# One encoder layer by Strassen quarters: a finished quarter is queued two steps later, the first W2 chunk reloads a tile, and the last chunk runs in another order

## The chip, the cores and the metric

The kernel runs on one core of a Trainium2 chip. The metric is the time of one execution on the device in microseconds (us). Times are given as a median of several runs; a profile is one more execution, taken by the hardware profiler.

## What is computed

One layer of a bidirectional encoder, 512 tokens of width 2048, all in float32. Only the second half matters here: the gate, the two feed-forward matrices and the last layer norm.

```python
mix = concat([rms_norm(A), rms_norm(B)]) @ w_o
h   = layer_norm(ALPHA * x + mix, ln1_g, ln1_b)
ff  = square(relu(h @ w1)) @ w2                  # w1: 2048 x 8192, w2: 8192 x 2048
ple = (p @ w_ple) * sigmoid(h @ w_ple_gate)      # w_ple_gate: 2048 x 2048
out = layer_norm(ALPHA * h + ff + ple, ln2_g, ln2_b)
```

## The kernel before

**Number format.** A float32 product is made of three matmuls (L653, L655, L656): each operand is split into a rounded part and the remainder (`wh`, `wl` for weights; `sh`, `sl` for the other side). ScalarE (ACT) makes the rounded part, VectorE (DVE) the remainder (L598, L599 for weights).

**Chunks and steps.** The three big matrices are worked off in chunks, each of them one call of `strassen` (L602): two chunks for the gate, eight for W1, then four pairs (`m` = 0 to 3, `c` = 0, 1) for W2; eighteen in all. A chunk multiplies a 512 x 1024 block by a 1024 x 1024 block with Strassen's (Winograd's) seven products instead of eight. Each block is cut into four quarters; product `p` (1 to 7) is accumulated over four depth slices `k` (0 to 3). A pair (p, k) is a **step**: 12 matmuls of 512 columns. The 28 steps of a chunk run in the order of `STEPS` (L804), counted here from 0 to 27. The results gather in three PSUM tiles `a`, `b`, `c` (`CHAIN`); when a product's last slice is done, `read` adds the PSUM tile into the output quarters. A quarter is finished after product 3, 7, 4 or 2 (`LAST`): in `STEPS` these end at step 18 (first half of the rows, second half of the columns), 19 (second, second), 25 (second, first) and 27 (first, first).

**Weight factors.** `factor(p, k)` (L609) loads the four weight quarters of slice k (each a 512 KB DMA) and forms the sums that the seven products need: at p = 1 it loads the first quarter (tag `r`), the second one (tag `q`, or `g` if `hold`) and the fourth one (tag `k`, issued from the POOL queue; all others come from the SP queue). At p = 5 it forms second minus first (L616) and the next sum (L617); at p = 3 it loads the fourth quarter again and, without `hold`, the second one again (L624), and forms their difference (L625). With `hold` (all W2 chunks) the second quarter stays in a `g` tile from p = 1 to p = 3 and is loaded once. At p = 2 and p = 4 the third quarter is loaded and the last sum formed (L634).

**Buffers.** `WB` (L803) gives the number of buffers of each tag, 512 KB each: `r` 4, `q` 2, `k` 4, `wh` 3, `wl` 3, `c` 3, `g` 4. `q` also takes the tiles `qs` through which the other side's factors for W2 come back from the scratch tensor `s_d` (`f_factors`, L576, L584); ten of them are placed at steps 3 to 21 of the chunk before a pair, four (`LATE`, L807) at steps 12, 14, 16 and 18 of the pair's first chunk. `g` takes the blocks `f` of the squared activations in W1, and the gate's side loads.

**What happens with a finished quarter.** `quarters(done)` (L661) calls `done` as soon as the quarter's last read is issued (L673). In the gate, `gated` (L683) loads two blocks, applies the sigmoid, transposes on TensorE (L694) and writes to `z_d`. In W1, `squared` (L705) transposes the quarter on TensorE into the tile `pt` (eight transposes, L710), applies relu and square on ACT, forms the sums that Strassen needs on the other side (L720 to L727) and writes seven factors to `s_d`. In W2 the results are added to `z_d` by DMA, but for the last pair (`m` = 3), where `last_sum` (L735) loads `z_d`, adds the PSUM tiles (L743) and takes the layer norm's statistics (L746).

**The end.** `finish(th, z)` (L761) works on one half of the rows (two tiles of 128 rows): per tile it loads the other columns, combines the statistics (L767), takes the reciprocal root by a short chain of tiny DVE operations (L269 to L277), applies two fused operations to three pieces (L777, L778) and stores them. In the last chunk it is called after product 4 (step 25, second half of the rows) and after product 2 (step 27, first half).

**What sets the order.** The framework's scheduler writes each engine's instruction stream, the DMA queues' too, when the program is built. It goes by program order among the instructions that it expects to be ready at that moment, so a load can be issued well ahead of its step as soon as a buffer of its tag is free, and an instruction that is not expected to be ready is passed by later ones. On the chip each engine then runs its stream strictly in order.

Of the kernel before, what the change touches and what calls it, by code (L numbers as in the profile page):

```python
# [11 lines left out]
F32 = mybir.dt.float32  # L12
# [5 lines left out]
P = 128  # L18
# [20 lines left out]
def block_kernel(ctx: ExitStack, tc: tile.TileContext, xT, pT, positions, w_in, w_o, w_gate, w_ple,  # L39
# [562 lines left out]
    def strassen(src, sg, read, hold=False, between={}):  # L602
# [4 lines left out]
        b11, b12, b21, b22, t2 = {}, {}, {}, {}, {}  # L607

        def factor(p, k):  # L609
            if p == 1:  # L610
                b11[k] = w_load(src(k, 0), "r")
                b12[k] = w_load(src(k, 1), "g" if hold else "q")
                t2[k] = w_load(src(k, 3), "k")
                return b11[k]
            if p == 5:
                nc.vector.tensor_tensor(b11[k], b12[k], b11[k], op=ALU.subtract)  # L616
                nc.vector.tensor_tensor(t2[k], t2[k], b11[k], op=ALU.subtract)  # L617
                return b11[k]
            if p == 6:
                return t2[k]  # L620
            if p == 3:
                b22[k] = w_load(src(k, 3), "r")
                if not hold:
                    b12[k] = w_load(src(k, 1), "q")  # L624
                nc.vector.tensor_tensor(b12[k], b22[k], b12[k], op=ALU.subtract)  # L625
                return b22[k]
            if p == 7:
                return b12[k]
            if p == 2:
                b21[k] = w_load(src(k, 2), "r")  # L630
                return b21[k]
            if k not in b21:
                b21[k] = w_load(src(k, 2), "r")
            nc.vector.tensor_tensor(t2[k], b21[k], t2[k], op=ALU.subtract)  # L634
            return t2[k]

        for n, (p, k) in enumerate(STEPS):
# [3 lines left out]
            if p == 2 and k in b21:  # L641
                wh, wl = w_split(b21[k])
            else:
                wh, wl = w_split(factor(p, k))
# [15 lines left out]

    def quarters(done):  # L661

        c = {}

        def read(p, b):
# [6 lines left out]
            if p in LAST:  # L672
                done(*q, c[q])  # L673
# [58 lines left out]
    bs = [st.tile([P, 4, nc.vector.BN_STATS_DIM], F32, name=f"bs{t}", bufs=1) for t in range(NQ)]  # L732
    gb = []

    def last_sum(c):  # L735
        z = {}
# [4 lines left out]
        def read(p, b):  # L741
            q = READ[p]
            nc.vector.tensor_tensor(z[q], z[q], b, op=ALU.add)  # L743
            if p in LAST:
                for t in range(2):
                    nc.vector.bn_stats(bs[2 * q[0] + t][:, 2 * c + q[1]], z[q][:, t])  # L746
                if c == 0:
                    nc.gpsimd.dma_start(z_d[q[0], q[1]], z[q])
            if c == 1 and p == 5:
# [7 lines left out]
            if c == 1 and p in (4, 2):  # L757
                finish(1 if p == 4 else 0, z)
        return read

    def finish(th, z):  # L761
        for i in range(2):
# [3 lines left out]
            mv = st.tile([P, nc.vector.BN_AGGR_DIM], F32, name="mv")  # L766
            nc.vector.bn_aggr(mv, bs[t])  # L767
            v = st.tile([P, 1], F32, name="v")
            nc.vector.tensor_scalar(v, mv[:, 1:2], LN_EPS, None, op0=ALU.add)
            r = st.tile([P, 1], F32, name="r")  # L770
            rsqrt(r, v)
            rows = slice(t * P, (t + 1) * P)
            for y, n, k in ((x.rearrange("p n s -> p (n s)"), 0, 2), (z[th, 0][:, i], 2, 1), (z[th, 1][:, i], 3, 1)):
# [3 lines left out]
                nc.vector.scalar_tensor_tensor(y, y, mv[:, 0:1], g[:, o], op0=ALU.subtract, op1=ALU.mult)  # L777
                nc.vector.scalar_tensor_tensor(y, y, r, b[:, o], op0=ALU.mult, op1=ALU.add)  # L778
# [4 lines left out]
    for m in range(NM):  # L783
# [5 lines left out]
        for c in range(2):  # L789
# [5 lines left out]
            strassen(lambda k, q, m=m, c=c: w2[m, c, q, k], sf, read if more else last_sum(c), True, mid)  # L795
# [11 lines left out]
LATE = {2: (12, 16), 4: (14, 18)}  # L807
CHAIN = {1: ("a", True), 6: ("a", False), 7: ("a", False), 4: ("a", False), 5: ("b", True), 3: ("b", False),
# [93 lines left out]
```

## Time and profile before

| | |
|---|---|
| median of 3 runs | 2268.99 us (2266.04 to 2269.82) |
| the profiled execution | 2262.9 us |
| its span, first to last instruction | 2261.1 us |
| TensorE (PE) busy | 2144.7 us, 95% |
| VectorE (DVE) busy | 1612.5 us, 71% |
| ScalarE (ACT) busy | 1061.6 us, 47% |
| mean granted TensorE clock | 0.982 |

Times in the trace count from the start of the span. The eighteen chunks start at 740.22 (gate), 919.59 (W1) and 1576.63 (W2); the last matmul starts at 2232.30. Matmuls are pipelined: the profile gives each one a modelled duration of about 0.39 us, while they start about 0.23 us apart, so a busy TensorE still can lose time, and the distance between starts tells more than the busy share. The granted clock has two levels here, 1.0 (2.4 GHz) and 0.5 (1.2 GHz).

### The profile page before, as it was taken

The numbers are of one execution on the slowest core, as the hardware profiler recorded it, in microseconds if no ns is written. First come the engines' busy times: TensorE is split into PE (matmuls) and PEld (weight loads), VectorE is DVE, ScalarE is ACT, GpSimd is POOL, SyncE is SP. The second block draws the span as 40 slices with busy tenths as digits, with TensorE's granted clock in tenths as the row PEclk, the third lists the DMA queues.
The fourth block names the chain that finished last, engine by engine and source line by source line (L and its number), as shares of the span: only waits on it lengthen the run. The fifth ranks groups of instructions, "written<-read, shape, count | busy, mean of one in ns | idle before, by whom it ended". The sixth has DMA issues, their size and how long they took to land.

```text
span 2261.1 us, 26072 instructions
## 1 busy us (share of the span) xinstructions
PE 2144.7 (95%) x9672; PEld 1757.3 (78%) x9672; DVE 1612.5 (71%) x1969; ACT 1061.6 (47%) x1372; POOL 124.3 (5%) x192
## 2 busy tenths in 40 slices
PE   9999999999995799999999999998899999999994
PEld 7888888888884588888888888776777787787783
DVE  7666655566475988776876877777677776777787
ACT  5554444343234444454555455455445555455331
POOL 0000000000003000000000000000011011001000
PEclk9999999999998899999999999999999999999997
DMA  6212212224225775565565566567669679678552
GB/s 225 75 66 76 84 66 84 84 100 138 99 88 209 269 271 202 202 230 180 190 229 177 196 214 204 190 221 250 202 186 285 182 206 277 181 210 289 187 197 82
DMA packets 124544, 401.60 MB, mean 178 GB/s; under 512 B 13024, under 2 KB 24288, under 8 KB 124416
## 3 DMA queue, kind: packets, MB, share of 16 engines
q1 hardware_dynamic: 88544, 285.51, 36.7%
q0 software_dynamic: 23584, 85.06, 13.4%
q10 hardware_dynamic: 12288, 29.36, 3.5%
q8 instruction: 76, 1.25, 0.2%
q14 instruction: 52, 0.43, 0.1%
HBM read 329.63 MB, written 70.25 MB: 177 GB/s over the span
## 4 chain that ended last, share of the span: by engine, by line
PE 76%; DMA 9%; DVE 9%; issue 3%; ACT 2%; DVEq 0%; SPq 0%; ACTq 0%
PE u L72 9%; PE u L71 9%; PE a L656 9%; PE u L73 9%; PE a L653 9%; PE a L655 8%; DMA wr<-in_w 5%; PE b L656 4%; PE b L653 4%; PE b L655 4%; DVE wl L599 4%; PE c L656 2%; PE c L653 2%; PE c L655 2%; DMA qs<-s_d 2%
## 5 line engine op out<-in xcount | busy, mean ns | idle before, releaser
L598 ACT ACTIVATE wh<-wr 128x1024 fp32r<-128x1024 f32 x288 | 303.8, 1059 | 345.2 <-PE a L655 194.0
L599 DVE TENSOR_TENSOR wl<-wr,wh 128x1024 fp32r<-128x1024 f32 x288 | 350.2, 1221 | 96.5 <-ACT wh L598 93.3
L64 ACT ACTIVATE wh<-raw 128x512 fp32r<-128x512 f32 x216 | 135.7, 629 | 282.2 <-PE u L72 267.3
L65 DVE TENSOR_TENSOR wl<-raw,wh 128x512 fp32r<-128x512 f32 x216 | 150.8, 699 | 160.8 <-ACT wh L64 129.0
L598 ACT ACTIVATE wh<-wk 128x1024 fp32r<-128x1024 f32 x144 | 152.6, 1060 | 179.3 <-PE b L655 89.5
L71 PE MATMUL u<-xh,wh 128*128 128x512 f32 x576 | 227.8, 395 | 5.6 <-ACT xh L64 5.6
L73 PE MATMUL u<-xh,wl 128*128 128x512 f32 x576 | 225.7, 392 | 0.0
L72 PE MATMUL u<-xl,wh 128*128 128x512 f32 x576 | 225.6, 392 | 0.0
L599 DVE TENSOR_TENSOR wl<-wk,wh 128x1024 fp32r<-128x1024 f32 x144 | 175.6, 1222 | 66.2 <-ACT wh L598 66.1
L634 DVE TENSOR_TENSOR wk<-wr,wk 128x1024 f32<-128x1024 f32 x72 | 88.2, 1224 | 97.1 <-DMA wr<-in_w 91.2
L653 PE MATMUL a<-wh,s1h 128*128 128x512 f32 x288 | 114.8, 399 | 30.7 <-DMA qh<-h_d 29.3
L71 PEld LDWEIGHTS u<-xh,wh 128*128 128x128 f32 x576 | 108.9, 189 | 27.1 <-ACT xh L64 5.6
L653 PE MATMUL b<-wh,s5h 128*128 128x512 f32 x288 | 116.6, 405 | 12.1 <-ACT wh L598 12.1
L73 PEld LDWEIGHTS u<-xh,wl 128*128 128x128 f32 x576 | 108.7, 189 | 22.7
L656 PE MATMUL b<-wl,s5h 128*128 128x512 f32 x288 | 117.2, 407 | 9.3 <-DVE wl L599 9.3
L72 PEld LDWEIGHTS u<-xl,wh 128*128 128x128 f32 x576 | 108.9, 189 | 22.0 <-DVE xl L65 0.4
L656 PE MATMUL c<-wl,s2h 128*128 128x512 f32 x288 | 113.3, 393 | 6.0 <-DVE wl L599 5.7
L656 PE MATMUL b<-wl,s3h 128*128 128x512 f32 x288 | 113.5, 394 | 4.1 <-DVE wl L599 3.9
L656 PE MATMUL a<-wl,s1h 128*128 128x512 f32 x288 | 114.8, 399 | 2.4 <-DVE wl L599 2.4
L655 PE MATMUL b<-wh,s5l 128*128 128x512 f32 x288 | 115.5, 401 | 0.0
L653 PE MATMUL a<-wh,s7h 128*128 128x512 f32 x288 | 112.6, 391 | 2.9 <-ACT wh L598 2.9
L656 PE MATMUL a<-wl,s7h 128*128 128x512 f32 x288 | 113.0, 392 | 1.2 <-DVE wl L599 1.1
(243 smaller groups left out, 4933.4 us busy)
## 6 DMA issues: line engine op xcount, KB each, us to landing
wr<-in_w SPq DMA_DIRECT2D x192, 512.0 KB, 4.0
raw<-in_w_in SPq DMA_DIRECT2D x64, 512.0 KB, 3.6
wq<-in_w SPq DMA_DIRECT2D x64, 512.0 KB, 3.7
wk<-in_w POOLq DMA_DIRECT2D x64, 512.0 KB, 4.8
qs<-s_d SPq DMA_DIRECT2D x56, 512.0 KB, 4.9
z_d<-ev POOLq DMA_DIRECT2D x42, 512.0 KB, 7.2
raw<-in_w_o SPq DMA_DIRECT2D x32, 512.0 KB, 3.4
s_d<-f POOLq DMA_DIRECT2D x32, 512.0 KB, 5.2
```

The source lines that it names most:

```text
L64: nc.scalar.activation(hi, src, AF.Copy)
L65: nc.vector.tensor_tensor(lo, src, hi.bitcast(F32), op=ALU.subtract)
L71: nc.tensor.matmul(o, wh, ah, start=start, stop=False)
L72: nc.tensor.matmul(o, wh, al, start=False, stop=False)
L73: nc.tensor.matmul(o, wl, ah, start=False, stop=stop)
L598: nc.scalar.activation(hi, t, AF.Copy)
L599: nc.vector.tensor_tensor(lo, t, hi.bitcast(F32), op=ALU.subtract)
L634: nc.vector.tensor_tensor(t2[k], b21[k], t2[k], op=ALU.subtract)
L653: nc.tensor.matmul(o, sh[:, i, x], wh[:, c], start=first and k == 0 and j == 0, stop=False, skip_group_check=skip)
L655: nc.tensor.matmul(o, sl[:, i, x], wh[:, c], start=False, stop=False, skip_group_check=skip)
L656: nc.tensor.matmul(o, sh[:, i, x], wl[:, c], start=False, stop=k == 3 and j == 1, skip_group_check=skip)
```

## The change

1. **Two steps later.** `quarters` no longer calls `done` at once; it puts it on a list `after`, and `strassen` runs it at the start of the second step from there. The quarters that end at steps 25 and 27 are thus handled at step 27 and at step 1 of the next chunk. `last_sum` does not use the list.
2. **Loads by need.** `factor` loads the second and fourth quarters at p = 5 instead of p = 1, two to three steps later in program order, in all chunks, and keeps every tile in a dictionary so that the products may come in another order.
3. **The first W2 chunk** (`m` = 0, `c` = 0) runs without `hold`: its second quarter is loaded into `q` at p = 5 and loaded again into `q` at p = 3 (four more DMAs of 512 KB).
4. **The last chunk** runs in the order `ENDS`: after step 11 come products 2, 7 and 4, then 3 and the rest of 2. The second half of the rows is finished at step 21, the first half at steps 26 and 27. The fourth quarter is loaded a third time there (four more DMAs of 512 KB).
5. **Statistics** of a half's two row tiles are combined in one chain of tiny operations instead of two (`row_stats`).

```diff
@@ strassen @@
-        b11, b12, b21, b22, t2 = {}, {}, {}, {}, {}
+        b11, b12, b21, b22, t1, t2, t3, t4 = ({} for _ in range(8))
+
+        def get(b, k, q, tag):
+            if k not in b:
+                b[k] = w_load(src(k, q), tag)
+            return b[k]
+
+        def sum4(k):
+            if k not in t4:
+                t4[k] = t2[k]
+                nc.vector.tensor_tensor(t4[k], get(b21, k, 2, "r"), t2[k], op=ALU.subtract)
+            return t4[k]
+
+        def sum3(k, b):
+            x = b12[k] if hold else w_load(src(k, 1), "q")
+            nc.vector.tensor_tensor(x, b, x, op=ALU.subtract)
+            t3[k] = x
+            return x
 
         def factor(p, k):
             if p == 1:
-                b11[k] = w_load(src(k, 0), "r")
-                b12[k] = w_load(src(k, 1), "g" if hold else "q")
-                t2[k] = w_load(src(k, 3), "k")
-                return b11[k]
+                return get(b11, k, 0, "r")
             if p == 5:
-                nc.vector.tensor_tensor(b11[k], b12[k], b11[k], op=ALU.subtract)
-                nc.vector.tensor_tensor(t2[k], t2[k], b11[k], op=ALU.subtract)
-                return b11[k]
+                spent = k in b11
+                x, y = get(b11, k, 0, "r"), get(b12, k, 1, "g" if hold else "q")
+                get(t2, k, 3, "k")
+                t1[k] = x if spent else y
+                nc.vector.tensor_tensor(t1[k], y, x, op=ALU.subtract)
+                nc.vector.tensor_tensor(t2[k], t2[k], t1[k], op=ALU.subtract)
+                return t1[k]
...
             if p == 3:
-                b22[k] = w_load(src(k, 3), "r")
-                if not hold:
-                    b12[k] = w_load(src(k, 1), "q")
-                nc.vector.tensor_tensor(b12[k], b22[k], b12[k], op=ALU.subtract)
-                return b22[k]
+                x = w_load(src(k, 3), "r")
+                if k not in t3:
+                    sum3(k, x)
+                return x
             if p == 7:
-                return b12[k]
+                return t3[k] if k in t3 else sum3(k, w_load(src(k, 3), "r"))
...
-        for n, (p, k) in enumerate(STEPS):
+        for n, (p, k) in enumerate(steps or STEPS):
+            for w in list(after):
+                w[0] -= 1
+                if w[0] == 0:
+                    after.remove(w)
+                    w[1]()
             for f in between.get(n, ()):
                 f()
@@ quarters @@
             if p in LAST:
-                done(*q, c[q])
+                after.append([2, lambda: done(*q, c[q])])
@@ last_sum and finish @@
+    def row_stats(th):
+        mv = st.tile([P, 2, nc.vector.BN_AGGR_DIM], F32, name="mv")
+        for i in range(2):
+            nc.vector.bn_aggr(mv[:, i], bs[2 * th + i])
+        v = st.tile([P, 2], F32, name="v2")
+        nc.vector.tensor_scalar(v, mv[:, :, 1], LN_EPS, None, op0=ALU.add)
+        r = st.tile([P, 2], F32, name="r2")
+        rsqrt(r, v)
+        return mv, r
...
+            if p in LAST:
+                ends.append(q[0])
+                if c == 1 and ends.count(q[0]) == 2:
+                    finish(q[0], z)
...
-            if c == 1 and p in (4, 2):
-                finish(1 if p == 4 else 0, z)
@@ W2 loop @@
-            strassen(lambda k, q, m=m, c=c: w2[m, c, q, k], sf, read if more else last_sum(c), True, mid)
+            strassen(lambda k, q, m=m, c=c: w2[m, c, q, k], sf, read if more else last_sum(c), m + c > 0, mid,
+                     STEPS if more or c == 0 else ENDS)
...
+ENDS = STEPS[:12] + ((2, 0), (7, 0), (7, 1), (7, 2), (7, 3), (2, 1), (4, 0), (4, 1), (4, 2), (4, 3),
+                     (3, 0), (2, 2), (3, 1), (3, 2), (2, 3), (3, 3))
```

## Rows read from the trace of the kernel before

**Rows 1.** The page: its first line and the chain of waits by engine.

```profile
span 2261.1 us, 26072 instructions
...
PE 76%; DMA 9%; DVE 9%; issue 3%; ACT 2%; DVEq 0%; SPq 0%; ACTq 0%
```

**Rows 2.** Stretches cut at chunk starts: length, busy us (instructions) per engine, clock, DMA share, GB/s.

```profile
740.22:838.66 98.44, 89.26 (x360) 69.25 (x361) 87.09 (x79) 50.22 (x49) 2.12 (x4) 0.92 0.76 264
...
999.71:1080.43 80.72, 80.26 (x369) 66.08 (x368) 60.01 (x52) 41.41 (x45) 4.25 (x8) 1.00 0.58 202
...
1403.76:1486.06 82.30, 80.22 (x369) 66.09 (x368) 59.85 (x52) 41.43 (x45) 4.26 (x8) 1.00 0.57 199
1486.06:1576.63 90.57, 83.93 (x369) 66.84 (x368) 70.46 (x61) 50.81 (x56) 4.25 (x8) 0.98 0.70 244
1576.63:1669.36 92.73, 82.37 (x346) 66.26 (x344) 61.98 (x54) 40.12 (x40) 9.58 (x14) 0.94 0.70 207
...
2155.89:2232.70 76.81, 76.60 (x337) 62.80 (x335) 64.02 (x65) 27.51 (x26) 2.64 (x5) 1.00 0.35 124
2232.70:2261.10 28.40, 0.00 (x0) 0.00 (x0) 24.20 (x72) 0.00 (x0) 0.00 (x0) 0.58 0.39 148
```

**Rows 3.** The same view of seventeen smooth steps (204 matmuls) of a W1 chunk.

```profile
1006.34:1052.58 46.24, 46.24 (x206) 38.29 (x204) 36.15 (x32) 20.80 (x21) 1.59 (x3) 1.00 0.56 199
```

**Rows 4.** Timeline of PE: transposes of two finished quarters in a W1 chunk.

```profile
1054.94 1.09 PE L710 MATMUL pt<-ident,c 128*128 128x128 f32 x8 [0.39 <-DVE c L671]
...
1058.43 1.03 PE L710 MATMUL pt<-ident,c 128*128 128x128 f32 x8
1059.22 0.48 PE L655 MATMUL c<-wh,s2l 128*128 128x512 f32 x1
```

**Rows 5.** Timeline of PE at the seam of W1 and W2.

```profile
1581.21 1.44 PE L710 MATMUL pt<-ident,c 128*128 128x128 f32 x8 [2.15 <-DVE c L671]
...
1594.00 0.80 PE L653 MATMUL b<-wh,s5h 128*128 128x512 f32 x1 [6.91 <-ACT wh L598]
```

**Rows 6.** Timeline of SP's DMA queue at four places (gate start, W1, last W1 chunk, seam).

```profile
727.25 11.29 SPq L545 DMA_DIRECT2D qh<-h_d  x2
...
1084.59 0.33 SPq L592 DMA_DIRECT2D wq<-in_w  x1
...
1483.29 0.33 SPq L584 DMA_DIRECT2D qs<-s_d  x1
...
1587.16 8.49 SPq L592 DMA_DIRECT2D wg<-in_w  x4
```

**Rows 7.** Timeline of DVE at four places: sums that need a loaded tile.

```profile
1083.35 1.22 DVE L616 TENSOR_TENSOR wr<-wq,wr 128x1024 f32<-128x1024 f32 x1
...
1502.83 1.23 DVE L616 TENSOR_TENSOR wr<-wq,wr 128x1024 f32<-128x1024 f32 x1 [2.26 <-DMA wq<-in_w]
...
1546.28 1.23 DVE L625 TENSOR_TENSOR wq<-wr,wq 128x1024 f32<-128x1024 f32 x1 [1.01 <-DMA wq<-in_w]
...
1591.64 1.22 DVE L616 TENSOR_TENSOR wr<-wg,wr 128x1024 f32<-128x1024 f32 x1 [3.62 <-DMA wg<-in_w]
```

**Rows 8.** Stretch at the seam (columns as in rows 2).

```profile
1591.99:1598.82 6.83, 4.82 (x11) 3.62 (x12) 6.80 (x7) 3.06 (x3) 0.00 (x0) 0.50 0.91 348
```

**Rows 9.** Timeline of DVE: after a product 4, and from the last product 4 to the end.

```profile
2151.79 1.22 DVE L599 TENSOR_TENSOR wl<-wr,wh 128x1024 fp32r<-128x1024 f32 x1
2152.92 1.28 DVE L746 BATCH_NORM_STATS2 bs<-zl 128x6 f32<-128x512 f32 x2
...
2227.28 1.22 DVE L743 TENSOR_TENSOR zl<-zl,a 128x1024 f32<-128x1024 f32 x1 [0.63 <-PE a L656]
...
2229.74 0.38 DVE L767 BATCH_NORM_AGGREGATE mv<-bs 128x2 f32<-128x24 f32 x2
...
2255.71 1.41 DVE L778 SCALAR_TENSOR_TENSOR zl<-zl,r,gb 128x512 f32<-128x512 f32 x2
```

**Rows 10.** Groups of DVE instructions by line in that last stretch: busy us, mean ns.

```profile
L277 DVE SCALAR_TENSOR_TENSOR r<-rt,r 128x1 f32<-128x1 f32 x12 | 1.6, 153 | 0.1
```

More of the change, by code (lines that the diff above doesn't have):

```diff
@@ L600, in w_split, with strassen @@
         return hi, lo
-    def strassen(src, sg, read, hold=False, between={}):
+    def strassen(src, sg, read, hold=False, between={}, steps=None):
         bank = {c: ps.tile([P, 2, S], F32, name=c, tag=c, bufs=1) for c in "abc"}
-        b11, b12, b21, b22, t2 = {}, {}, {}, {}, {}
+        b11, b12, b21, b22, t1, t2, t3, t4 = ({} for _ in range(8))
[13 more added lines that the diff above has]
+            return x
         def factor(p, k):
             if p == 1:
-                b11[k] = w_load(src(k, 0), "r")
-                b12[k] = w_load(src(k, 1), "g" if hold else "q")
-                t2[k] = w_load(src(k, 3), "k")
-                return b11[k]
+                return get(b11, k, 0, "r")
             if p == 5:
-                nc.vector.tensor_tensor(b11[k], b12[k], b11[k], op=ALU.subtract)
-                nc.vector.tensor_tensor(t2[k], t2[k], b11[k], op=ALU.subtract)
-                return b11[k]
+                spent = k in b11
[5 more added lines that the diff above has]
+                return t1[k]
             if p == 6:
@@ L621, in factor @@
             if p == 3:
-                b22[k] = w_load(src(k, 3), "r")
-                if not hold:
-                    b12[k] = w_load(src(k, 1), "q")
-                nc.vector.tensor_tensor(b12[k], b22[k], b12[k], op=ALU.subtract)
-                return b22[k]
+                x = w_load(src(k, 3), "r")
+                if k not in t3:
+                    sum3(k, x)
+                return x
             if p == 7:
-                return b12[k]
+                return t3[k] if k in t3 else sum3(k, w_load(src(k, 3), "r"))
             if p == 2:
[L630 to L635, printed above, removed]
-        for n, (p, k) in enumerate(STEPS):
+                return get(b21, k, 2, "r")
+            return sum4(k)
+        for n, (p, k) in enumerate(steps or STEPS):
[4 more added lines that the diff above has]
+                    w[1]()
             for f in between.get(n, ()):
@@ L640, in strassen @@
             chain, first = CHAIN[p]
[L641 to L644, printed above, removed]
+            wh, wl = w_split(factor(p, k))
             sh, sl = sg[k // 2][p]
@@ L659, in strassen @@
                 read(p, bank[chain])
+    after = []
     def quarters(done):
@@ L732, in block_kernel @@
     bs = [st.tile([P, 4, nc.vector.BN_STATS_DIM], F32, name=f"bs{t}", bufs=1) for t in range(NQ)]
+    def row_stats(th):
[7 more added lines that the diff above has]
+        return mv, r
     gb = []
     def last_sum(c):
-        z = {}
+        z, ends = {}, []
         for q in ((0, 0), (1, 1), (0, 1), (1, 0)):
```

11 lines of the change are left out of this document (3 added, 8 removed).

## Prediction

> **What bounds the kernel now.** I read the page first. The span is 2261.1 us and the chain that ended last is 76% TensorE [rows 1]. The layer norms, the attention and the wait at the start of the gate are not touched, so I went on to a table of stretches cut at the chunk starts [rows 2] and held each chunk against what its matmuls need. Seventeen smooth steps, 204 matmuls, take 46.24 us [rows 3], so 336 matmuls take 76.2. A W1 chunk also holds four groups of eight transposes. One group takes 0.79 us to the next matmul, and that matmul shows 0.48 instead of the usual 0.39 [rows 4], so 0.9 in all, and the floor of a W1 chunk is 76.2 + 3.6 = 79.8. Against that the table shows four kinds of chunk. A plain W1 chunk takes 80.7 (one row stands; the five from the second to the sixth lie between 80.72 and 80.88, the first takes 80.12): TensorE is the bound and only 0.9 is to be had. The seventh takes 82.30. The last W1 chunk takes 90.57 and the first W2 chunk 92.73, where the floor is 76.2 + 0.9 = 77.1: there other things bind. The last chunk takes 76.81, and behind its end lie 28.40 us without a matmul, in which DVE is busy for 24.20. The first gate chunk, 98.44 at a DMA share of 0.76, is bound by transfers.
>
> **Part 1, a finished quarter two steps later.** In the W1 chunks the transposes stand in PE's stream shortly behind the product that finishes the quarter, and there they wait for the addition L671: 0.39 in a plain chunk, while the next group waits for nothing [rows 4], and 2.15 at the seam of W1 and W2 [rows 5]. Two steps are 5.4 us and the addition takes 1.2, so the wait goes even when DVE comes to it late. Gain over the first seven W1 chunks: 0.3 + 5 x 1.0 + 2.5 = 7.8, and about 0.7 in the second gate chunk (80.93 by the same view, with 36 transposes). I take 8, since a little of it is restart behind the transposes. What is moved with the quarter: two relus and a square on ACT, the four sums L720 to L727 on DVE, one transfer on ACT's queue and up to four on POOL's. They come 5.4 us later, into the first steps of the next chunk, where DVE also forms L616 and L617; DVE is busy for 60.0 of 80.7 us of a chunk [rows 2], which is the cover. If it did not hold, half a microsecond per chunk would be the price: bounds -9 and +5. The `c` tiles live two steps longer; the next chunk wants its first one at step 5, the last old one is spent at step 1, so nobody waits. On POOL's queue the weight loads that follow wait for `k` buffers that are given back only from step 21 on.
>
> **Part 2, the seam.** The first W2 chunk loses 92.73 - 77.1 = 15.6. The view of PE shows two waits: 2.15 for L671 and 6.91 for a weight factor [rows 5]. Behind the second one stands a chain: the last quarter's blocks `f` occupy `g`, so SP can issue the four loads `wg` only from 1587.16 on [rows 6], and L616 on DVE sits 3.62 waiting for the first of them [rows 7]. The waits bring the clock down: it is at 0.50 from 1591.99 to 1598.82 and few matmuls start there [rows 8]. With the change neither wait has a cause: the quarter's transposes come two steps later, and the second quarter goes into `q`, which is free once the last W1 chunk has spent its own (at its steps 17 and 19). So the 15.6 go. What comes in their place: eight tiles (four second quarters, four `qs`) pass the two `q` buffers around steps 8 to 19. The nearest row is the last W1 chunk, in which ten `qs` and eight second quarters share them: it loses 90.57 - 79.8 = 10.8, first where L616 waits 2.26 for a `q` tile, then at the sums L625, one of which waits 1.01 [rows 7]. Bounds for the new cost are thus 0 and 10.8. I take 4, an estimate: only the steps from 12 on are repeated, to which I give half of that loss, and four `qs` come there instead of five. Net -11.6, bounds -15.6 and -4.8. The four extra loads come at a DMA share of 0.70 [rows 2] and take the place of idle time.
>
> A rule of the Trainium skill speaks against this part: Perfetto Trace Analysis, Identifying the Most-Contended Engine, says that a gap that repeats on the engine that should be saturated can mean that buffers are too few for the next tile. By it the loss of the last W1 chunk would come back whole, and the sum below would be about 7 smaller.
>
> **Part 3, loads two or three steps later in program order.** What decides when a load is issued is its buffer: in a plain chunk `wq` is issued at 1084.59 [rows 6], just as L616, begun at 1083.35 with 1.22 to run [rows 7], gives its buffer back. That does not change, so I cost it at nothing in the plain chunks; the cover is the freed buffer's lead over its use. Two places differ. In the last W1 chunk the first `qs` (issued at 1483.29 now [rows 6]) outranks the second quarter of slice 1 and will take a `q` buffer earlier and hold it; then the other loads pass one buffer for a while. That may double the stall of 2.26 with its clock loss (+4) or shift it away (-4); I take 0, as the tile that L616 waits for comes at about the same time. At the start of the gate SP stands 11.29 behind loads `qh` without a buffer [rows 6]; the first `wq` was issued ahead of that and now falls behind it, while the first-quarter loads move forward. The bytes are the same and transfers bind there: 0, bounds -5 and +5. The seven later W2 chunks: 0, -3 to +3.
>
> **Part 4, the last chunk and the end.** From the last addition of product 4 at 2227.28 to the end of the last operation, 2255.71 + 1.41 = 2257.12, DVE works without a break for 29.8 us [rows 9], and the span ends 4.0 later. With `ENDS` the same point, the end of product 4, comes four steps (10.9 us) earlier. DVE's list behind it then has one more addition with its statistics (2.5, from 2227.28 to 2229.74 [rows 9]), four weight splits that used to lie ahead of it (1.13 apart [rows 9], so 4.5), and half of the tiny operations less: there are 36 in the root's steps, 12 of them 1.6 us [rows 10], with 16 others about 7 us of overlapping work, so I take 2.5 off. Gain: 10.9 - 2.5 - 4.5 + 2.5 = 6.4. This holds if DVE stays the bound, which asks that PE gets its splits in time: after an addition a split comes before the statistics [rows 9], and the root's chain leaves further gaps. If instead all of `finish` went ahead of them, PE would stand about 9 us and the gain would be nought, or -3 with a clock loss. I take 6.2, bounds 6.6 and -3. The four extra loads lie in a stretch with a DMA share of 0.35 [rows 2]. On SP's queue the stores of the second half now come among the loads of the last steps, and a store that waits for L778 holds up what is behind it; those loads' `r` buffers come free before the first L778, so I cost this at nothing, with the 9 us of PE above as the price if they don't.
>
> **Sum.** -8 - 11.6 - 6.2 = -25.8. The profiled execution took 2262.9, its span of 2261.1 and 1.8 around it, so it would become 2237.1. It lies 6.1 below the median of the runs, 2269.0; the forecast is set on the median: 2269.0 - 25.8 = 2243.
>
> **Rivals.**
> *Two buffers are too few.* The first W2 chunk behaves like the last W1 chunk (net -4.8) and that one gets worse by 4: -8 - 4.8 + 4 - 6.2 = -15, so 2254. For it: the waits of L616 and L625 on `wq` [rows 7]. Against: fewer `qs`, and their factor buffers are long free. 0.2. (The rule of the Trainium skill cited above, in Perfetto Trace Analysis, points this way.)
> *The deferral changes nothing*, since the scheduler already lets matmuls pass the transposes: in rows 4 one of two groups waits for nothing. Then -17.8, so 2251. Against: the waits of 0.39 and 2.15. 0.1.
> *The end gives nothing*: `finish` on DVE ahead of the splits starves PE in the last steps, and what is won is lost there. -19.6, or -16.6 with a clock loss: 2249 to 2252. 0.1.
> *Slower: the later loads bind in every chunk.* If a load goes by its place rather than by its buffer, L616 waits at the start of each chunk as it does once now, 2.26 [rows 7]; sixteen chunks by 2.3 are 37 us, net +11, so 2280. It decides from 1.9 per chunk on. For it: that wait is in the trace where `q` is crowded. Against: the issue at 1084.59 [rows 6]. 0.09.
>
> **How the numbers follow.** The forecast has 0.5; its own bounds, with a gate start 5 better and the seam at its best, reach 2231. The first three rivals are all faster; two of them together give about 2262, so the range ends at 2264. What lies above it is the slower rival and the case that all three come true. About 0.2% (4.5 us) can be told from no change: faster means under 2264.5, slower over 2273.5. Faster 0.83, same 0.08, slower 0.09.
>
> **What would show it.** Right: no wait of L710 for L671 and plain W1 chunks of about 79.9; the first W2 chunk at about 81 with the clock at 1.0 and no wait at its second and fourth step; the last chunk at about 77 and some 22 us behind it. Wrong: a first W2 chunk over 88 with L616 or L625 waiting for `wq`; W1 chunks above 81 with L616 waiting at their start; gaps of several us between the last steps while L777 and L778 run; a first gate chunk over 104.

## The result, and the profile after

The changed kernel takes 2252.84 us (median of 4 runs, 2249.11 to 2253.21) against 2269.16 for the kernel before on the same chip: a ratio of 0.9927 with a 95% interval of 0.991 to 0.9944. It is faster by 16, where 26 were forecast; the time is within the range and 9.8 over the forecast of 2243. The profiled execution took 2253.21, its span 2251.4. That is 9.7 less than the span of before and not 16, since the profile of before came from a quick execution, as the prediction said. A second profile of before (the first experiment) lies 3.6 higher; single chunks move by a microsecond or two from one execution to the next.

The first line of the page after, and its chain by engine, answer to [rows 1]:

```profile
span 2251.4 us, 26067 instructions
...
PE 76%; DMA 9%; DVE 9%; issue 4%; ACT 2%; DVEq 0%; SPq 0%; ACTq 0%
```

The page alone tells nothing: the same shares. The table of stretches does, with the columns of [rows 2]: the first gate chunk, the second W1 chunk, the seventh, the eighth (last), the first W2 chunk, the last chunk, what lies behind it:

```profile
740.87:839.05 98.18, 89.39 (x361) 69.30 (x361) 87.05 (x80) 49.67 (x50) 2.11 (x4) 0.92 0.78 265
1000.18:1079.91 79.73, 79.73 (x369) 66.37 (x368) 59.61 (x52) 41.36 (x45) 4.25 (x8) 1.00 0.62 205
1399.95:1480.75 80.80, 79.96 (x370) 66.30 (x368) 59.52 (x52) 41.48 (x45) 4.25 (x8) 1.00 0.60 202
1480.75:1577.19 96.44, 87.38 (x370) 68.85 (x368) 71.53 (x62) 50.15 (x55) 4.25 (x8) 0.95 0.67 224
1577.19:1663.13 85.94, 81.47 (x346) 65.54 (x344) 61.10 (x53) 40.55 (x41) 9.55 (x14) 0.96 0.82 254
2151.05:2228.17 77.12, 76.73 (x337) 62.72 (x335) 67.69 (x78) 27.49 (x26) 2.64 (x5) 1.00 0.44 154
2228.17:2251.41 23.24, 0.00 (x0) 0.00 (x0) 18.83 (x35) 0.00 (x0) 0.00 (x0) 0.56 0.45 169
```

Against [rows 2]: a plain W1 chunk went from 80.72 to 79.73, its floor; the seventh from 82.30 to 80.80. The first W2 chunk gained 6.8, the end behind the last matmul 5.2. But the **last W1 chunk lost 5.9**: 96.44 for 90.57, with the clock at 0.95 for 0.98. The first seven W1 chunks together gave 6.1, so the account of the two profiles reads -6.1 + 5.9 - 6.8 - 5.2, and the rest (gate, other W2 chunks, last chunk) +2.5: -9.7.

**The other W1 chunks** do not wait at their start. Two groups of DVE from 920 to 1475 us (busy us, mean ns, idle before):

```profile
L617 DVE TENSOR_TENSOR wk<-wr,wk 128x1024 f32<-128x1024 f32 x28 | 34.3, 1225 | 31.8 <-DMA wr<-in_w 31.8
...
L634 DVE TENSOR_TENSOR wr<-wq,wr 128x1024 f32<-128x1024 f32 x27 | 32.4, 1220 | 0.2
```

L634 is the L616 of before; in 27 of them it waits 0.2 in all. L617, which needs the third quarter, waits 31.8 in all for loads, in chunks that stay within 1.0 of their floor. (L625 is now L622, L671 is L689, and the matmuls L653 to L656 are L668 to L671.)

**Where the last W1 chunk stands.** The timeline of SP's queue of the changed kernel, to be held against [rows 6]:

```profile
1450.27 0.33 SPq L584 DMA_DIRECT2D qs<-s_d  x1
...
1490.61 0.33 SPq L592 DMA_DIRECT2D wq<-in_w  x1
```

The timeline of DVE there:

```profile
1489.36 1.22 DVE L533 TENSOR_TENSOR s1l<-qs,s1h 128x1024 fp32r<-128x1024 f32 x1
...
1497.83 1.23 DVE L634 TENSOR_TENSOR wr<-wq,wr 128x1024 f32<-128x1024 f32 x1 [3.84 <-DMA wq<-in_w]
...
1507.14 1.23 DVE L634 TENSOR_TENSOR wr<-wq,wr 128x1024 f32<-128x1024 f32 x1 [1.93 <-DMA wq<-in_w]
```

The timelines of ACT and of PE, one row each:

```profile
1499.14 1.06 ACT L598 ACTIVATE wh<-wr 128x1024 fp32r<-128x1024 f32 x1 [8.30 <-DVE wr L634]
```

```profile
1500.26 0.64 PE L668 MATMUL b<-wh,s5h 128*128 128x512 f32 x1 [2.05 <-ACT wh L598]
```

Read it from the top. The first `qs` is issued at 1450.27, 30.5 before its chunk begins at 1480.75; in the kernel before it came 2.8 ahead of it (1483.29). It takes one of the two `q` buffers and is not spent until the remainder at 1489.36 has read it. Right after that, at 1490.61, SP can issue the second quarter of the third slice, and L634 waits 3.84 for it; one round later it waits 1.93 again. ACT, next in the chain, has stood 8.30, and TensorE waits. The sum of the fourth slice, the one that waited 2.26 before, begins 26.4 into the chunk (1507.14); before, it began 16.8 into it (1502.83 [rows 7]).

How large the loss is, one trace does not settle. Three of the later runs keep these loads and this early `qs`; their last W1 chunks take 94.39, 93.60 and 93.80. The first of them (`e3_steps_last`) has the same instructions in SP's queue up to its last chunk. Its stretch:

```profile
1483.86:1578.25 94.39, 84.38 (x369) 66.65 (x368) 71.48 (x62) 49.84 (x55) 4.27 (x8) 0.98 0.68 228
```

Its mean clock is 0.98, where the changed kernel's trace has 0.95. If TensorE's work goes with the clock, an estimate from that column (0.05 of 96.44 against 0.02 of 90.57) is that about 3 of the 5.9 are the clock and the rest waits. Against the kernel before, the four traces put the loss at 3 to 6.

**Where the first W2 chunk stands.** The timeline of PE in the changed kernel, its first transposes and its stall:

```profile
1579.91 1.03 PE L728 MATMUL pt<-ident,c 128*128 128x128 f32 x8
...
1600.05 0.79 PE L668 MATMUL a<-wh,s6h 128*128 128x512 f32 x1 [2.77 <-ACT ev L817]
```

The timeline of ACT ahead of it:

```profile
1598.03 1.06 ACT L532 ACTIVATE s2h<-qs 128x1024 fp32r<-128x1024 f32 x1 [5.25 <-DMA qs<-s_d]
1598.99 1.00 ACT L817 ACTIVATE ev<-a 128x1024 f32<-128x1024 f32 x1
```

The stretch around the stall, columns as in [rows 2]:

```profile
1594.00:1606.00 12.00, 9.23 (x29) 7.09 (x28) 6.73 (x6) 4.72 (x5) 0.89 (x1) 0.73 0.95 340
```

Both waits of [rows 5] are gone. In their place ACT stands 5.25 in front of the split of a late `qs`, behind which its stream holds the copy L817 that frees a PSUM tile; TensorE waits for that copy and runs the stretch at a mean clock of 0.73.

**The end.** The timeline of DVE in the changed kernel: the addition of product 4 and the four weight splits behind it, the last addition, the last operation:

```profile
2211.75 1.22 DVE L771 TENSOR_TENSOR zl<-zl,a 128x1024 f32<-128x1024 f32 x1 [0.63 <-PE a L671]
2212.89 1.22 DVE L599 TENSOR_TENSOR wl<-wr,wh 128x1024 fp32r<-128x1024 f32 x1
...
2215.38 1.18 DVE L599 TENSOR_TENSOR wl<-wr,wh 128x1024 fp32r<-128x1024 f32 x1
...
2222.05 1.22 DVE L599 TENSOR_TENSOR wl<-wr,wh 128x1024 fp32r<-128x1024 f32 x1
...
2223.25 1.22 DVE L599 TENSOR_TENSOR wl<-wr,wh 128x1024 fp32r<-128x1024 f32 x1
...
2231.55 1.22 DVE L771 TENSOR_TENSOR zl<-zl,b 128x1024 f32<-128x1024 f32 x1
...
2245.83 1.41 DVE L803 SCALAR_TENSOR_TENSOR zl<-zl,r,gb 128x512 f32<-128x512 f32 x2
```

From 2211.75 to the end of the last operation, 2245.83 + 1.41 = 2247.24, DVE works without a break for 35.5; before it was 29.8 from the same point [rows 9], but the point now comes 16.4 ahead of the last matmul's end at 2228.2 and no longer 5.4.

### The profile page after: what moved, and what is told of

It reads as the page before. It is cut to its first block, busy times and chain, and to the rows that moved or that the text cites. A ratio compares the mean times of both kernels' runs of the same rounds, so it can differ in the third digit from the quotient of the medians.

```text
span 2251.4 us, 26067 instructions
## 1 busy us (share of the span) xinstructions
PE 2144.6 (95%) x9672; PEld 1760.2 (78%) x9672; DVE 1608.7 (71%) x1945; ACT 1060.3 (47%) x1372; POOL 124.3 (6%) x192
## 4 chain that ended last, share of the span: by engine, by line
PE 76%; DMA 9%; DVE 9%; issue 4%; ACT 2%; DVEq 0%; SPq 0%; ACTq 0%
PE u L71 9%; PE u L72 9%; PE u L73 9%; PE a L668 9%; PE a L670 8%; PE a L671 8%; PE b L671 4%; DVE wl L599 4%; PE b L668 4%; PE b L670 4%; DMA wr<-in_w 4%; PE c L671 2%; PE c L668 2%; PE c L670 2%; DMA qs<-s_d 2%
## 5 line engine op out<-in xcount | busy, mean ns | idle before, releaser
L617 DVE TENSOR_TENSOR wk<-wr,wk 128x1024 f32<-128x1024 f32 x72 | 88.1, 1224 | 90.5 <-DMA wr<-in_w 83.5
L668 PE MATMUL a<-wh,s1h 128*128 128x512 f32 x288 | 114.7, 398 | 31.4 <-ACT wh L598 31.2
L668 PE MATMUL b<-wh,s5h 128*128 128x512 f32 x288 | 116.3, 404 | 8.4 <-ACT wh L598 8.4
L671 PE MATMUL b<-wl,s5h 128*128 128x512 f32 x288 | 117.1, 407 | 7.3 <-DVE wl L599 7.3
L668 PE MATMUL a<-wh,s6h 128*128 128x512 f32 x288 | 113.8, 395 | 4.9 <-ACT ev L817 2.8
L671 PE MATMUL b<-wl,s3h 128*128 128x512 f32 x288 | 113.2, 393 | 5.0 <-DVE wl L599 4.9
L671 PE MATMUL c<-wl,s2h 128*128 128x512 f32 x288 | 113.2, 393 | 4.9 <-DVE wl L599 4.7
L668 PE MATMUL a<-wh,s7h 128*128 128x512 f32 x288 | 113.0, 392 | 4.4 <-ACT wh L598 4.1
L671 PE MATMUL a<-wl,s1h 128*128 128x512 f32 x288 | 113.7, 395 | 2.4 <-DVE wl L599 2.4
```

The costliest lines, as they stand in the source:

```text
L617: nc.vector.tensor_tensor(t4[k], get(b21, k, 2, "r"), t2[k], op=ALU.subtract)
L668: nc.tensor.matmul(o, sh[:, i, x], wh[:, c], start=first and k == 0 and j == 0, stop=False, skip_group_check=skip)
L671: nc.tensor.matmul(o, sh[:, i, x], wl[:, c], start=False, stop=k == 3 and j == 1, skip_group_check=skip)
```

## The experiments

Each starts from the changed kernel unless it says otherwise. Lengths are of the profiled execution in us: the seven first W1 chunks together, the last W1 chunk, the first W2 chunk, and the end, counted from 0.23 behind the start of the last matmul (the stretch shown above begins 0.17 later). Ratios stand against the kernel before, run on the same chip in the same batch. Across batches the ratios compare better than the times: in the batches of the experiments the kernel before took 2265.3, 2268.8 and 2269.0.

| | time | ratio (95%) | W1, 7 | W1 last | W2 first | end |
|---|---|---|---|---|---|---|
| before | 2269.16 | 1 | 566.5 | 90.57 | 92.73 | 28.60 |
| after | 2252.84 | 0.9927 (0.991 to 0.9944) | 560.4 | 96.44 | 85.94 | 23.41 |
| `e1_load_at_1` | 2243.01 | 0.9899 (0.9883 to 0.9915) | 560.1 | 90.01 | 84.04 | 23.40 |
| `e2_no_delay` | 2256.45 | 0.9956 (0.9939 to 0.9973) | 566.9 | 93.60 | 84.08 | 23.41 |
| `e3_steps_last` | 2254.01 | 0.9942 (0.9928 to 0.9957) | 560.4 | 94.39 | 84.87 | 27.33 |
| `e5_qs_later` | 2245.03 | 0.9892 (0.987 to 0.9914) | 560.3 | 88.28 | 85.23 | 23.45 |
| `e6_hold_3` | 2247.36 | 0.9901 (0.9878 to 0.9923) | 559.2 | 90.51 | 84.79 | 23.49 |
| `e7_late_later` | 2239.38 | 0.987 (0.9849 to 0.9891) | 561.3 | 91.30 | 79.87 | 23.43 |
| `e8_both` | 2243.86 | 0.9886 (0.9861 to 0.9911) | 559.7 | 88.80 | 82.01 | 23.45 |
| `e9_qs_both` | 2241.35 | 0.9878 (0.986 to 0.9896) | 561.7 | 87.05 | 79.83 | 23.43 |
| `e10_qs_both_load_1` | 2238.49 | 0.9864 (0.9847 to 0.9882) | 560.8 | 85.98 | 79.69 | 23.39 |
| `e11_hold` | 2259.79 | 0.996 (0.9948 to 0.9972) | 561.8 | 93.80 | 92.01 | 23.65 |

**The kernel before, once more.** 

> The kernel before once more, for a second trace. The two profiled executions differ by 9.7 us (2262.9 and 2253.2), the medians of the runs by 16.3 (2269.2 and 2252.8). Theory 1: the profiled execution of before was a quick one, and some stretch that the change does not touch differs between executions; then this one takes 2266 to 2270 and one or two stretches ahead of the gate, or with a clock at half, are 3 to 7 us longer than in the first trace. Theory 2: the profile itself changes the time; then its profiled execution is again near 2263 and its timed one near 2269.

It took 2266.56, its span 2264.8: the last W1 chunk 90.25, the first W2 chunk 93.25. Most of the 3.6 that it is longer than the first profile lies in the first gate chunk (1.1), the seventh W1 chunk (1.6) and one late W2 chunk (2.2). So the account above is good to about 2 per chunk. Neither theory fits whole: the profiled execution lies among the other runs of before in its batch (2265.0 to 2269.1), which gives no sign that the profile changes the time; but the surplus is spread, and no chunk holds 3 of it.

**The loads back at product 1** (undoes part 3 of the prediction):

```diff
             if p == 1:
-                return get(b11, k, 0, "r")
+                get(b11, k, 0, "r")
+                get(b12, k, 1, "g" if hold else "q")
+                get(t2, k, 3, "k")
+                return b11[k]
```

> Undoes part 3 alone: the second and fourth weight quarters are loaded at p = 1 again in all chunks, all else as changed. Rival 'two buffers are too few' in its form 'the place of the load decides who gets a q buffer': the last W1 chunk goes from 96.4 back to 90 or 91, the waits of L634 for wq in it (3.84 and 1.93) shrink to about 2 in all, the rest stays: 2253 - 6 = 2247. Forecast's step 'a load goes by its buffer, its place costs nothing': all chunks within 1 us of the changed kernel, 2253, and the last W1 chunk's 5.9 us more come from transfers that land later (wq took 7 us there).

The timeline of SP's queue around the start of the last W1 chunk in this run:

```profile
1450.84 0.33 SPq L592 DMA_DIRECT2D wq<-in_w  x1
...
1478.31 0.33 SPq L584 DMA_DIRECT2D qs<-s_d  x1
```

Its table of stretches, that chunk and the next:

```profile
1481.07:1571.08 90.01, 82.11 (x369) 65.80 (x368) 71.04 (x62) 50.04 (x55) 4.25 (x8) 1.00 0.70 239
1571.08:1655.12 84.04, 78.55 (x345) 63.44 (x344) 61.15 (x53) 40.66 (x41) 9.55 (x14) 1.00 0.81 260
```

The second quarter takes the buffer at 1450.84 and the first `qs` comes at 1478.31, as in the kernel before. The last W1 chunk is back at 90.0, the time is 10 lower by the medians (by the ratios 0.28%, some 6). The first W2 chunk is 1.9 shorter too, which was not expected. Part 3 is thus a loss, and this version beats both kernels, the changed one by little more than the noise (the intervals overlap from 0.991 to 0.9915). It does not tell yet whether the place of the loads or the order in the `q` buffers is the cause.

**No delay** (undoes part 1):

```diff
-                after.append([2, lambda: done(*q, c[q])])
+                done(*q, c[q])
```

> Undoes part 1 alone: a finished quarter is handled at once, all else as changed (the first W2 chunk still loads its second quarter twice). Theory that the two steps took the waits of the transposes: plain W1 chunks go from 79.8 back to 80.7, the seventh from 80.8 to 82.3, sum +6, and the first W2 chunk from 85.9 to 88 or 89 with a wait of L728 for L689 of about 2 us: 2253 + 8 = 2261. Rival 'the deferral changes nothing': within 2 us of 2253.

The first seven W1 chunks take 566.9, as before the change, against 560.4: 6.5 for part 1, and the interval of the ratio lies above that of the changed kernel but for a sliver (0.9939 to 0.9944). The first W2 chunk does not get longer. The timeline of PE at that seam in this run shows its transposes, which come at once and wait for nothing:

```profile
1576.75 1.05 PE L728 MATMUL pt<-ident,c 128*128 128x128 f32 x8
...
1583.11 1.06 PE L728 MATMUL pt<-ident,c 128*128 128x128 f32 x8
```

So the delay did not take away the 2.15 of [rows 5] at the seam.

**The old order in the last chunk** (undoes `ENDS`, keeps the joint statistics):

```diff
-                     STEPS if more or c == 0 else ENDS)
+                     STEPS)
```

> Undoes part 4 but for the joint statistics: the last chunk runs in the old order, the second half of the rows ends at step 25, the first at step 27, and the root's chain is shared by two tiles. Theory that the order gave the end's gain: behind the last matmul 28.4 - 2.5 = 26 us instead of 23.2, the last chunk 76.8: 2253 + 2.5 = 2255.5. Rival: the joint statistics gave most of it; then 23 to 24 us stay behind the last matmul and the time is 2253.

The stretch behind the last matmul in this run:

```profile
2225.83:2252.99 27.16, 0.00 (x0) 0.00 (x0) 22.51 (x49) 0.00 (x0) 0.00 (x0) 0.57 0.41 155
```

The end grows by 3.9 (27.33 for 23.41 in the table) and stays 1.3 under that of before. The order is worth 3.9; the other 1.3 are put down to the joint chain of tiny operations, by difference, as no run undoes it alone. The rival, 23 to 24 us, is out. The time moves by 3.4 by the ratios and by 1.2 by the medians; in the profile the last W1 chunk and the first W2 chunk are shorter here, though the edit does not reach them.

**The ten `qs` of the last W1 chunk later**, the loads left at product 5:

```diff
-                at[late].setdefault(LATE[p][g] if late else STEPS.index((p, 2 * g + 1)) + 2, []).append(step)
+                at[late].setdefault(LATE[p][g] if late else STEPS.index((p, 2 * g + 1)) + (2 if m else 5), []).append(step)
```

> The changed kernel with the loads left at product 5, but the ten blocks `qs` of the last W1 chunk five steps behind their product's last use instead of two. Theory (a `qs` of slice group 0 takes a `q` buffer at 1450 ahead of the second quarter of slice 1 and holds it until 1489, so that the other tiles pass one buffer): the second quarter gets its buffer back, the last W1 chunk falls from 96.4 to 92 or less, nothing else moves but a little in the first W2 chunk, whose factors come later: about 5 us less than the changed kernel. Rival (the last W1 chunk is longer because its loads stand later in the program order, whoever shares the buffers): it stays within 1.5 of 96.4 and the time within 2 us of the changed kernel's, or longer, since the `qs` now crowd into the end of the chunk.

The timeline of SP's queue in this run:

```profile
1453.48 0.33 SPq L592 DMA_DIRECT2D wq<-in_w  x1
...
1480.98 0.33 SPq L584 DMA_DIRECT2D qs<-s_d  x1
```

DVE's only wait of L634 there, in its timeline:

```profile
1502.57 1.23 DVE L634 TENSOR_TENSOR wr<-wq,wr 128x1024 f32<-128x1024 f32 x1 [0.91 <-DMA wq<-in_w]
```

The stretch of its last W1 chunk:

```profile
1483.74:1572.02 88.28, 83.40 (x370) 66.94 (x369) 70.65 (x62) 50.36 (x55) 4.27 (x8) 0.98 0.72 244
```

The `qs` has moved from 1450 to 1481, the waits of 3.84 and 1.93 are one of 0.91, and the chunk takes 88.28 with its loads where the change put them. The theory of the buffer's order stands, the rival falls. The time is 7.8 lower by the medians and as much by the ratios.

**What is left of the first W2 chunk.** Three runs on the kernel with its loads at product 1. The first gives slice 3's second quarter a `g` buffer, the second asks for the four late `qs` later, the third does both:

```diff
-                x, y = get(b11, k, 0, "r"), get(b12, k, 1, "g" if hold else "q")
+                x, y = get(b11, k, 0, "r"), get(b12, k, 1, "g" if k in hold else "q")
...
-            strassen(lambda k, q, m=m, c=c: w2[m, c, q, k], sf, read if more else last_sum(c), m + c > 0, mid,
+            strassen(lambda k, q, m=m, c=c: w2[m, c, q, k], sf, read if more else last_sum(c), range(4) if m + c else (3,), mid,
```

```diff
-                at[late].setdefault(LATE[p][g] if late else STEPS.index((p, 2 * g + 1)) + 2, []).append(step)
+                at[late].setdefault((LATE if m else LATE0)[p][g] if late else STEPS.index((p, 2 * g + 1)) + 2, []).append(step)
...
 LATE = {2: (12, 16), 4: (14, 18)}
+LATE0 = {2: (16, 24), 4: (18, 22)}
```

> The changed kernel with the loads back at product 1, and in the first W2 chunk the second quarter of slice 3 alone in a `g` buffer. The question is what is left of that chunk's loss (84.0 with the loads at product 1, floor 77.1). Theory Q (too many tiles for two `q` buffers): one tile of eight goes elsewhere, the second late `qs` and the additions behind it come sooner, the chunk falls to 81 to 82 and the time by 2 to 3 us against the run with the loads at product 1. Theory A (ScalarE stands 6 us behind the first late `qs`, because that split is placed ahead of weight splits that could run): the place of that split does not change, so the chunk stays at 83 to 85.

The timeline of ACT in the first of the three, its two waits for a late `qs`:

```profile
1580.05 1.06 ACT L532 ACTIVATE s2h<-qs 128x1024 fp32r<-128x1024 f32 x1 [1.68 <-DMA qs<-s_d]
...
1602.95 1.06 ACT L532 ACTIVATE s4h<-qs 128x1024 fp32r<-128x1024 f32 x1 [6.58 <-DMA qs<-s_d]
```

The stretch of its first W2 chunk:

```profile
1570.98:1655.76 84.78, 80.00 (x345) 64.64 (x344) 60.86 (x53) 40.70 (x41) 9.61 (x14) 0.98 0.83 251
```

One tile less in `q` does not help: the chunk stays at 84.8, and the ratio (0.9901) is that of the run with the loads at product 1 (0.9899). The first late `qs` now waits little, contrary to what the second theory said, but the next one holds ACT for 6.58.

> The changed kernel with the loads back at product 1, and in the first W2 chunk alone the four late `qs` at steps 16, 18, 22 and 24 instead of 12, 14, 16 and 18. Theory A (ScalarE stands 6 us behind the first late `qs` at 1586.7 to 1592.7, with a copy of a product and weight splits behind it): the wait goes, TensorE does not stop at its sixth to eighth step, and the chunk falls from 84.0 to 80 or 81, the time by 3 to 4 us. Theory Q (two `q` buffers for eight tiles, wherever they are asked for): the stall moves to the last products, which use these factors from step 20 on, and the chunk stays at 83 or more, or gets longer.

SP's queue issues the first late `qs` in the second of the three 33.2 into the chunk, at 1607.52; in the changed kernel it was 13.3 into it:

```profile
1607.52 0.33 SPq L584 DMA_DIRECT2D qs<-s_d  x1
```

ACT splits it without a wait:

```profile
1611.58 1.04 ACT L532 ACTIVATE s2h<-qs 128x1024 fp32r<-128x1024 f32 x1
```

The stretch of that chunk:

```profile
1574.36:1654.23 79.87, 78.02 (x345) 63.51 (x344) 60.94 (x53) 40.62 (x41) 9.61 (x14) 1.00 0.86 273
```

The chunk takes 79.87, the clock is 1.00, no stall comes back later, and all that at the highest DMA share of these runs, 0.86. So neither the number of buffers nor the transfers by themselves set that stall: it came with ACT standing in front of a `qs` whose data had not landed. The edit moves two things at once, the request for the buffer and the place of the split, and no run separates them; that in the first of the three ACT's wait moved to the next late `qs`, and TensorE's longest wait (2.8) with it, speaks for the split. 2239.4 is 13 under the changed kernel and 3.6 under the run with the loads at product 1 by the medians (some 7 by the ratios).

> Both edits of the first W2 chunk together on the kernel with the loads back at product 1: the second quarter of slice 3 in `g`, and the four late `qs` later. If either theory holds alone, this is as fast as the better of the two; if the stall needs both causes (a load that comes late and an engine that waits for it in order), only this one brings the chunk to about 79 and the time some 5 us under that of the run with the loads at product 1. If the chunk stays at 83 to 85 here as well, neither the buffers nor the place of the `qs` set it, and the transfers that crowd there (a DMA share of about 0.9) are what is left.

No gain from both: the chunk takes 82.01, where 79.87, the better of the two, was the least that was expected. The timeline of DVE in the third run shows a wait for another tile, the fourth quarter:

```profile
1597.48 1.23 DVE L622 TENSOR_TENSOR wg<-wr,wg 128x1024 f32<-128x1024 f32 x1 [3.90 <-DMA wr<-in_w]
```

Why that load is late was not followed further.

**Both sets of `qs` later**, with the loads at product 5 and then at product 1:

```diff
-                at[late].setdefault(LATE[p][g] if late else STEPS.index((p, 2 * g + 1)) + 2, []).append(step)
+                at[late].setdefault((LATE if m else LATE0)[p][g] if late else STEPS.index((p, 2 * g + 1)) + (2 if m else 5), []).append(step)
```

> The changed kernel as it is (loads at product 5), with both sets of `qs` later: those of the last W1 chunk five steps behind instead of two, the four late ones of the first W2 chunk at steps 16, 18, 22 and 24. Theory (what the change failed to gain at the seam is the order in which `qs` and second quarters take the two `q` buffers, in both chunks): the last W1 chunk at 88 to 90, the first W2 chunk at 80 to 81, so 96.4 + 85.9 falls by 12 to 14 and the time to about 2240; the loads at product 5 then cost nothing. Rival (the loads' place costs something of its own): the time stays 3 us or more above that of the same kernel with the loads at product 1, in the same batch.

> The same with the loads at product 1 again. Theory: no faster than with the loads at product 5, within 2 us, since the buffers' order is already set by the later `qs`; about 2238 and the last W1 chunk at 88 to 90. Rival: 2233 to 2236, the sum of both gains (10 by the loads, 5 by the later `qs` in the last W1 chunk).

The stretches of the last W1 and the first W2 chunk in the run with the loads at product 5:

```profile
1483.75:1570.80 87.05, 83.19 (x370) 66.87 (x369) 70.88 (x62) 50.63 (x55) 4.26 (x8) 0.98 0.72 247
1570.80:1650.62 79.82, 78.04 (x345) 63.54 (x344) 60.96 (x53) 40.62 (x41) 9.57 (x14) 1.00 0.86 274
```

These two chunks take 15.5 less than in the changed kernel, with the same buffers, the same bytes and the loads where the change put them. The changed kernel's trace was a long one in the last W1 chunk, as said above; with the last W1 chunk of the three other traces in its place the gain is 12.7 to 13.5. With the loads at product 1 the time is 2.9 less again, more than the 2 of the theory and just under the 3 of the rival, with intervals that overlap (0.986 to 0.9896, and 0.9847 to 0.9882) and a last W1 chunk of 85.98: whether the place of the loads costs something of its own once the `qs` ask later, up to about 3, stays open. 2238.5 is the best median of the study, though `e7_late_later` with 2239.4 can't be told from it. By the medians the two `qs` edits are worth 11.5 and not 15.5; in the profile the W2 chunks between the first and the last take 2.8 longer (490.76 for 487.92).

**The second quarters held in `g` again** (undoes part 2):

```diff
-            strassen(lambda k, q, m=m, c=c: w2[m, c, q, k], sf, read if more else last_sum(c), m + c > 0, mid,
+            strassen(lambda k, q, m=m, c=c: w2[m, c, q, k], sf, read if more else last_sum(c), True, mid,
```

> The changed kernel with the second quarters of the first W2 chunk held in `g` as before; the delay of two steps stays. Theory (the gain of that chunk, 92.7 to 85.9, is all the second quarter's place): the wait for `wg` comes back, the chunk takes 91 to 94, the time is 5 to 8 us above the changed kernel's. Rival (half of it is the delay, since with the transposes two steps later the blocks `f` are copied out at another time): the chunk stays at 88 to 90, or, if the blocks give `g` back 5 us later for the delay, it takes 96 to 98.

The timeline of DVE at the seam in this run:

```profile
1593.43 1.23 DVE L634 TENSOR_TENSOR wr<-wg,wr 128x1024 f32<-128x1024 f32 x1 [4.44 <-DMA wg<-in_w]
```

That of PE:

```profile
1582.49 1.07 PE L728 MATMUL pt<-ident,c 128*128 128x128 f32 x8 [1.42 <-DVE c L689]
1595.80 0.79 PE L668 MATMUL b<-wh,s5h 128*128 128x512 f32 x1 [9.50 <-ACT wh L598]
```

The stretch of its first W2 chunk:

```profile
1578.19:1670.20 92.01, 80.76 (x345) 65.14 (x344) 61.85 (x54) 39.92 (x41) 9.57 (x14) 0.94 0.70 209
```

The waits of [rows 5, 7] are back, 9.50 where 6.91 stood, and the chunk takes 92.01. The reload in `q` is worth 6.1 in the chunk and 7 in the time (7.5 by the ratios); the wait of the transposes at the seam also stays, with the delay in place (1.42). Both waits at the seam hung on the hold.

## Why the prediction was right and where it was wrong

**Right: the sign, the range, and three of the four mechanisms.** The first four W1 chunks fell to their floor (79.73 to 79.83), the next three to 80.2 to 80.8, the first W2 chunk's waits for `wg` and for L671 went, and DVE kept TensorE supplied at the end with the four splits threaded through `finish`. The slower rival is out: in seven W1 chunks L634 waits 0.2 in all. The first gate chunk, where the loads changed places with `qh`, took 98.18 for 98.44, the zero that was taken.

**The step that failed is part 3: "I take 0, as the tile that L616 waits for comes at about the same time."** It did not. The prediction saw that the first `qs` would outrank a second quarter and hold its buffer, and named the place, but it put it at nothing between bounds of -4 and +4. Measured: the fourth slice's sum comes 9.6 later in the chunk, and the chunk takes 5.9 more, outside the bounds; in the three other traces with the same loads 3.0 to 3.8 more, inside them. Undoing the loads (90.01) or letting the `qs` ask later (88.28) takes it back whole. The bound was sized by doubling a stall of 2.26. What decided is for how long the buffer was held. The `qs` came at 1450 and lay there until 1489, since its two splits stand in the next chunk's part of ACT's and DVE's streams, so two rounds of loads went through one buffer and L634 waited 3.84 and 1.93.

**Part 2 was mis-sized: net -11.6 forecast, -6.8 in the chunk** (-6.1 against the run with the hold). The old loss did go; what came in its place was 8.8 (85.94 less the floor of 77.1) and not 4. The prediction looked for it at the sums L616 and L625, from step 12 on. The larger part came at steps 6 to 8 and by another way: it had counted the late `qs` as users of a buffer, and left out the split of each that stands in ACT's stream with a PSUM copy behind it. Of that 8.8, 6.1 went with the `qs` asking later; about 3.4 of it was the clock (an estimate, 0.04 of 85.94). The delay of part 1 was also credited with the 2.15 at the seam; the run without it shows no wait there.

**Rival one, "Two buffers are too few", gave the number (2254) but not the reason.** Its terms were +4 in the last W1 chunk and -4.8 in the first W2 chunk, measured +5.9 and -6.8, so that two errors of about 2 cancel: the number is luck. With the same two buffers the chunks reach 87.1 and 79.8. The rule that the prediction weighed is in the Trainium skill, Perfetto Trace Analysis, section Optimization Strategy (the prediction names the section in front of it): a gap that repeats can mean too few buffers. Here the gap came, and in the first W2 chunk the trace does not agree with that cause, since another order of asking closed it to 2.7 over the floor. In the last W1 chunk the runs leave it open: 87.1 is still 7.3 over the floor of 79.8, and DVE still waits for `q` tiles there, at L622 in the run with both sets of `qs` later:

```profile
1532.87 1.23 DVE L622 TENSOR_TENSOR wq<-wr,wq 128x1024 f32<-128x1024 f32 x1 [1.07 <-DMA wq<-in_w]
1534.87 1.22 DVE L622 TENSOR_TENSOR wq<-wr,wq 128x1024 f32<-128x1024 f32 x1 [0.77 <-DMA wq<-in_w]
```

A third `q` buffer was not tried.

**Part 1** was forecast at 8 and gave 6.1 in seven chunks (8.6 against the second profile of before, 6.5 in the run without it); the 0.7 of the second gate chunk did not come (81.33 for 80.92). **Part 4** was forecast at 6.2 and gave 5.2 behind the last matmul, with the last chunk 0.3 longer. The terms 10.9, 2.5 and 4.5 fit; the joint statistics were put at 2.5 and gave 1.3. A likely reason, not tested, is that many of the tiny operations cost little, as they alternate with large ones (L777 and L743 in the trace of before). 10.9 - 2.5 - 4.5 + 1.3 is 5.2.

The shortfall against the sum of -25.8, in the profiles: part 1 2.3 with the gate's, part 2 4.8, part 3 5.9, part 4 1.3, the other chunks 1.8, in all 16.1. The medians leave 9.8, since the profile of before was a quick run. In the range, the lower end of 2231 does not follow from the two terms named for it (2243 - 5 - 4 is 2234).

## What to carry to other kernels

When tiles of two kinds share a tag, moving one kind later in program order can hand the buffer to the other, and here the price came from how long the new holder kept it: look up when the holder is spent before calling such a move free. A load that arrives late can cost next to nothing (L617 above: 31.8 of waits in chunks near their floor); it cost where an engine that runs its stream in order had other work behind it that the next engine needed, so place its consumer no earlier than its data can be there. Where a chunk with crowded buffers stalls, try another order of asking before another buffer: here it gave 11.5 us by the medians.

## What the runs showed of the hardware

A wait of ACT of about the same length cost differently. In the run with the loads at product 1 ACT stood longer in front of the same split:

```profile
1592.66 1.06 ACT L532 ACTIVATE s2h<-qs 128x1024 fp32r<-128x1024 f32 x1 [5.99 <-DMA qs<-s_d]
```

TensorE then waited 3.5 for the copy behind it, and yet the whole first W2 chunk stayed at a clock of 1.00 and took 84.04. In the changed kernel the two waits were 5.25 and 2.77, but the mean clock was 0.96, 0.73 in the 12 us around the stall, and the chunk took 85.94. Why the clock fell in one and not in the other, the runs do not show. The largest DMA share among the first W2 chunks shown, 0.86 at 273 and 274 GB/s, is that of the two chunks without this stall: a high share alone did not make it.
